# Prompt attention and the sample tokens' cache units as one 16-step software pipeline, with TensorE, VectorE and ScalarE held to the order of the text

## The chip, the cores and the metric

The kernel runs on one core of one Trainium2 chip. The metric is the device time of one execution in microseconds (us). The engines are called PE (TensorE, matrix products and transposes), DVE (VectorE), ACT (ScalarE), POOL (GpSimd, which here issues indirect DMA copies) and SP (SyncE, which issues the other DMA copies). Each engine works through its own queue in order and waits on semaphores that other engines and DMA transfers raise.

## The reference, cut to what matters

One layer of a hybrid decoder: a half-step FFN, a token mixer with 4 GLA heads and 4 MLA heads, an output projection, a second half-step FFN. The change touches the MLA heads only: causal attention of a prompt of 1024 positions, and attention of 8 sample tokens over 4096 cached positions each, which lie in pages.

```python
def mla_prompt_attention(q_nope, q_pe, lat, k_pe, w_uk, w_uv):
    k_nope = jnp.einsum('btc,chd->bthd', lat, w_uk)
    v = jnp.einsum('btc,chd->bthd', lat, w_uv)
    ...
        s = (jnp.einsum('bqhd,bkhd->bhqk', qn, k_nope)
             + jnp.einsum('bqhr,bkr->bhqk', qp, k_pe)).astype(jnp.float32) * MLA_SCALE
        s = jnp.where(kpos[None, :] <= qpos[:, None], s, -jnp.inf)
        p = jax.nn.softmax(s, axis=-1)
        return jnp.einsum('bhqk,bkhd->bqhd', p.astype(v.dtype), v)

def mla_sample_attention(past_lat, past_pe, q_nope, q_pe, lat, k_pe, w_uk, w_uv):
    lat_all = jnp.concatenate([past_lat.astype(lat.dtype), lat], axis=1)
    pe_all = jnp.concatenate([past_pe.astype(k_pe.dtype), k_pe], axis=1)
    q_lat = jnp.einsum('bqhd,chd->bqhc', q_nope, w_uk)
    s = (jnp.einsum('bqhc,bkc->bhqk', q_lat, lat_all)
         + jnp.einsum('bqhr,bkr->bhqk', q_pe, pe_all)).astype(jnp.float32) * MLA_SCALE
    p = jax.nn.softmax(s, axis=-1)
    o_lat = jnp.einsum('bhqk,bkc->bqhc', p.astype(lat_all.dtype), lat_all)
    return jnp.einsum('bqhc,chd->bqhd', o_lat, w_uv).reshape(B, T, MLA_WIDTH)
```

## The kernel before

Every fp32 operand of a prompt product is split into two parts that the PE takes at one pass each: `split` (L90 on ACT for the upper part `_h`, L91 on DVE for the rest `_l`), and `mm3` (L99) adds three products of such parts. The stage concerned begins after the last GLA transpose (L976, `on`) and ends at the first matmul of the output projection (`pr<-ym_h`, L99), which reads the attention's result `ym`.

**Prompt.** The loops run over pairs of heads `t`, heads `hh` and blocks `m` of 256 queries; `scores(m)` projects the queries (`ps<-qn`, then `q_h`, `q_l`), and for each of two row tiles of 128 queries multiplies with keys up to the diagonal in chunks of at most 512 (`sc`, L1381 to L1387: five matmuls and, on the diagonal, a mask), takes the maximum (L1389), the exponential with its sum (L1396), the reciprocal (L1401), and multiplies by it (L1402, DVE). `outputs` of the block before transposes the probabilities (L1417), splits them (`pT_h`, `pT_l`) and multiplies by the values (`po`), and the result is split into `ym`. A pair of heads starts with its rotary queries (`rope`: four ACT copies `sw`, three DVE operations, then `qs`), its values `v` and, for each head, its keys `k`.

**Sample tokens.** 16 units `(g, u)`: four tokens times one eighth of the cache. `prepare` issues eight indirect copies on POOL (L1169: four of `kvt`, four of `pet`) and four DVE transposes in blocks of 32 (`kT` L1171, `peT` L1173). `dec_unit` multiplies (L1198, 48 small matmuls), takes maximum and exponential (L1182, L1183), transposes the probabilities by matmuls with a selector (L1204, 32), copies them on ACT (L1205, `dpT`), multiplies by the cache (L1208, 32) and copies out (L1209, `oc`). `decode(2)` runs two units ahead of the prompt; after that `decode(1)` stands behind each block `m`. `prepare` of the next unit is called behind each unit; tiles `kvt` and `pet` have three buffers, of which a unit takes two.

**Order.** The text gives the dependencies; within them a scheduler decides by its own model in which order the instructions stand in each engine's queue, with `high_priority` on the splits of `pT`. Behind the attention come the GLA results: `yraw` is loaded (its buffer is held by a one-element POOL copy until a block of head 2 is done, L1461), split into `yg`, and then the first tiles of `w_out` are split (`wh`, `wl`). The tiles `raw` (four buffers) are shared by all these loads.

Of the kernel before, what the change touches and what calls it, by code (L numbers as in the profile page):

```python
# [10 lines left out]
F32 = mybir.dt.float32  # L11
# [5 lines left out]
OP = mybir.AluOpType  # L17
# [56 lines left out]
def hybrid_step(ctx: ExitStack, tc: tile.TileContext, I, O, C):  # L74
# [1068 lines left out]
    uv = ep.tile([P, 4, P], F32, name="uv", bufs=1)  # L1143
    ld.dma_start(uv, w_uv)
# [42 lines left out]
    def dec_unit(g, u):  # L1187

        if u == 0:
            grp[g] = (ep.tile([P, 3, NU + 1], F32, name="stat", tag="stat"), ep.tile([P, NU + 1, P], F32, name="oc", tag="oc", bufs=1))  # L1190
        oc = grp[g][1]
        kvs, kts, pts = ready.pop((g, u))
        d = dbank("dsc")
        sc, pTp, po = d[:, :P], d[:, P:384], d[:, 384:]
        steps = [(qbl, kts, cb) for cb in range(4)] + [(qbp, pts, cb) for cb in range(2)]
        for n, (q_, k_, cb) in enumerate(steps):
            for bi in range(4):
                PE.matmul(sc[rows[bi]].rearrange("p (j k) -> p j k", j=J), q_[:, 4 * g + bi, cb], k_[bi][:, :, 32 * cb:32 * cb + 32],  # L1198
                          start=n == 0, stop=n == 5)
        pp = ep.tile([P, P], F32, name="dpp", tag="dpp")  # L1200
        softmax(g, u, sc, P, pp)
# [3 lines left out]
        S.activation(dpT.rearrange("p j t r -> p (j t) r")[:, :, :16], pTp.rearrange("p (x r) -> p x r", r=16), AF.Copy)  # L1205
        for j in range(J):
            for bi in range(4):
                PE.matmul(po[rows[bi]], dpT[:, j, bi], kvs[bi][:, j], start=j == 0, stop=j == J - 1)  # L1208
        S.activation(oc[:, u], po, AF.Copy)  # L1209

    def dec_combine(g):
# [3 lines left out]
        for bi in range(4):  # L1215
            b = 4 * g + bi
            PE.matmul(p[rows[bi], :NS], qlp[:, b], lat_s, start=True, stop=False)
            PE.matmul(p[rows[bi], :NS], qpp[:64, b], kp_s, start=False, stop=True)
        sn = ep.tile([P, NS], F32, name="sn", tag="sn")
        V.tensor_add(sn, p[:, :NS], newmask[:, g * NS:(g + 1) * NS])  # L1220
        pn = ep.tile([P, NS], F32, name="pn", tag="pn")
        softmax(g, NU, sn, NS, pn)
        p = dbank()
        PE.transpose(p[:NS, :P], pn, ident)
        pnT = ep.tile([NS, P], F32, name="pnT", tag="pnT", bufs=1)
        V.tensor_copy(pnT, p[:NS, :P])
        p = dbank()
        PE.matmul(p[:, :P], pnT, latn_s, start=True, stop=True)
        V.tensor_copy(oc[:, NU], p[:, :P])

# [4 lines left out]
        V.transpose(cx[1], cx[0])  # L1235
        V.tensor_reduce(cx[2][:, 16:20], cx[1][:, :16].rearrange("p (a h) -> p h a", h=4), AX.X, OP.min)
        V.tensor_copy(cx[2][:, :16].rearrange("p (a h) -> p a h", h=4),
                      cx[2][:, 16:20].rearrange("p (o h) -> p o h", o=1).to_broadcast([P, 4, 4]))
        V.transpose(cx[3], cx[2])

        S.activation(stat[:, 2, :], stat[:, 0, :], AF.Exp, bias=cx[3][:, 0:1], scale=-1.0)
        V.tensor_mul(stat[:, 1, :], stat[:, 1, :], stat[:, 2, :])
        V.tensor_reduce(cx[2][:, 20:21], stat[:, 1, :], AX.X, OP.add)
# [18 lines left out]
    def decode(n):  # L1262

        for _ in range(min(n, len(units))):
            g, u = units.pop(0)
            dec_unit(g, u)
            if units:
                prepare(*units[0])
# [417 lines left out]
```

## Time and profile before

| what | value |
|---|---|
| median of 3 runs | 2151.42 us (2149.89 to 2153.05) |
| profiled execution | 2162.53 us, span 2160.7 us |
| PE busy | 2013.9 us, 93% |
| DVE busy | 1500.4 us, 69% |
| ACT busy | 818.6 us, 38% |
| POOL busy | 194.2 us, 9% |

The span is the traced part of the profiled execution; busy times are shares of it. Times in the trace count from the span's start. "Idle before" names what a waiting engine waited for; "remote" is a completion of another engine whose instruction had ended earlier than its semaphore came, "issue" a time in which nothing is shown that the engine waited for. PEclk is the clock granted to the PE, as a share of full speed.

### The profile page before, as it was taken

How to read it: one execution, taken by the hardware profiler on the slowest of the kernel's cores; microseconds unless marked ns; L12 is line 12 of the kernel's file. 1: busy time of each engine (PE TensorE's matmuls, PEld its weight loads, DVE VectorE, ACT ScalarE, POOL GpSimd, SP SyncE). 2: the span in 40 equal slices, each digit the busy share in tenths (PEclk: the TensorE clock that was granted, in tenths of full speed). 3: DMA queues.
4: the chain of work that ended last, by engine and by line, in shares of the span. 5: the costliest groups of instructions: out<-in, count | busy, mean ns of one | idle time of the engine just before them, and what ended most of it. 6: DMA issues, size and time to landing. Idle time of an engine off the chain costs nothing. (4 is left out here: it accounts for less than half of the span.)

```text
span 2160.7 us, 41324 instructions
## 1 busy us (share of the span) xinstructions
PE 2013.9 (93%) x16808; PEld 1909.6 (88%) x16808; DVE 1500.4 (69%) x2925; ACT 818.6 (38%) x1555; POOL 194.2 (9%) x225
## 2 busy tenths in 40 slices
PE   7999999999999999897477778899999999999997
PEld 7999999999999988886255657699999999999997
DVE  6877777784968575765455556477777777776776
ACT  6423323244446223456322434344332232333534
POOL 1000000000000012112543341000000000000000
PEclk9999999999999999999688899899999999999999
DMA  6232232377445321022422331643332332475352
GB/s 205 71 121 91 88 123 84 94 228 237 133 130 147 84 73 32 21 88 63 140 83 80 103 104 59 191 147 113 108 90 87 119 94 87 145 259 165 115 154 94
DMA packets 205438, 251.31 MB, mean 116 GB/s; under 512 B 23352, under 2 KB 165984, under 8 KB 205248
## 3 DMA queue, kind: packets, MB, share of 16 engines
q1 hardware_dynamic: 197056, 223.49, 33.6%
q0 software_dynamic: 8192, 25.17, 3.7%
q8 instruction: 132, 2.16, 0.4%
q14 instruction: 58, 0.48, 0.1%
HBM read 189.32 MB, written 59.30 MB: 115 GB/s over the span
## 5 line engine op out<-in xcount | busy, mean ns | idle before, releaser
L99 PE MATMUL pp<-bh,ah 128*128 128x260 f32 (+1 forms) x2432 | 688.0, 283 | 3.8 <-ACT bh L90 3.3
L99 PE MATMUL pp<-bl,ah 128*128 128x260 f32 (+1 forms) x2432 | 688.7, 283 | 1.3 <-DVE bl L91 1.3
L99 PE MATMUL pp<-bh,al 128*128 128x260 f32 (+1 forms) x2432 | 689.6, 284 | 0.2 <-DVE al L91 0.2
L99 PEld LDWEIGHTS pp<-bh,ah 128*128 128x128 f32 x2432 | 460.2, 189 | 4.1 <-ACT bh L90 3.5
L99 PEld LDWEIGHTS pp<-bl,ah 128*128 128x128 f32 x2432 | 459.3, 189 | 1.7 <-DVE bl L91 1.7
L99 PEld LDWEIGHTS pp<-bh,al 128*128 128x128 f32 x2432 | 459.5, 189 | 0.6 <-DVE al L91 0.6
L415 PE MATMUL pp<-tl,dh 128*128 128x256 f32 x1232 | 248.8, 283 | 0.1
L415 PE MATMUL pp<-th,dh 128*128 128x256 f32 (+1 forms) x1232 | 248.7, 283 | 0.0
L415 PE MATMUL pp<-th,dl 128*128 128x256 f32 x1232 | 248.5, 282 | 0.0
L90 ACT ACTIVATE ah<-raw 128x512 fp32r<-128x512 f32 x208 | 129.1, 628 | 258.6 <-PE pp L99 244.2
L415 PEld LDWEIGHTS pp<-tl,dh 128*128 128x128 f32 x1232 | 190.0, 188 | 2.5 <-DVE tl L91 2.4
L415 PEld LDWEIGHTS pp<-th,dh 128*128 128x128 f32 x1232 | 190.7, 189 | 0.1
L415 PEld LDWEIGHTS pp<-th,dl 128*128 128x128 f32 x1232 | 189.7, 188 | 0.2 <-DVE dl L91 0.2
L91 DVE TENSOR_TENSOR al<-raw,ah 128x512 fp32r<-128x512 f32 x208 | 142.4, 688 | 63.7 <-ACT ah L90 63.4
L90 ACT ACTIVATE dh<-a 128x1024 fp32r<-128x1024 f32 (+1 forms) x84 | 83.0, 989 | 249.5 <-PE pp L415 228.0
L91 DVE TENSOR_TENSOR dl<-a,dh 128x1024 fp32r<-128x1024 f32 (+1 forms) x84 | 95.2, 1134 | 113.8 <-ACT dh L90 107.3
L90 ACT ACTIVATE ah<-sl 128x512 fp32r<-128x512 f32 x132 | 83.1, 631 | 214.4 <-PE pp L99 162.2
L99 PE MATMUL pw<-xh,wh 128*128 128x260 f32 (+4 forms) x320 | 100.9, 315 | 0.0
L99 PE MATMUL pw<-xl,wh 128*128 128x260 f32 (+4 forms) x320 | 99.8, 312 | 0.0
L99 PE MATMUL pw<-xh,wl 128*128 128x260 f32 (+4 forms) x320 | 99.5, 311 | 0.0
L91 DVE TENSOR_TENSOR tl<-traw,th 128x1032 fp32r<-128x1032 f32 (+1 forms) x84 | 95.5, 1137 | 3.0 <-ACT th L90 2.7
L91 DVE TENSOR_TENSOR al<-sl,ah 128x512 fp32r<-128x512 f32 x132 | 90.4, 687 | 7.6 <-ACT ah L90 3.8
(433 smaller groups left out, 3642.6 us busy)
## 6 DMA issues: line engine op xcount, KB each, us to landing
traw<-td SPq DMA_DIRECT2D x70, 516.0 KB
raw<-in_ffn_w_gate_dram SPq DMA_DIRECT2D x52, 512.0 KB
raw<-in_ffn_w_up_dram SPq DMA_DIRECT2D x52, 512.0 KB
a<-in_ffn_w_down_dram SPq DMA_DIRECT2D x40, 512.0 KB
td<-q SPq DMA_DIRECT2D x22, 520.0 KB
td<-q SPq DMA_DIRECT2D x22, 512.0 KB
raw<-in_w_out_dram SPq DMA_DIRECT2D x16, 512.0 KB
td<-q SPq DMA_DIRECT2D x22, 260.0 KB
```

The lines of the kernel that those rows point to most:

```text
L90: S.activation(out_h, src, AF.Copy)
L91: eng.tensor_sub(out_l, src, out_h)
L99: PE.matmul(ps, w_, x_, start=i == 0, stop=i == n - 1)
L415: PE.matmul(bank[c][m], w_[:, kk, ms], x_[:, kk, c * N[0]:c * N[0] + N[c]], start=first and j == 0 and (c == 1 or m % 2 == 0), stop=last a ...
```

## The change

`prepare` becomes `fetch` (the eight copies) and `turn` (one DVE transpose); `kvt` gets four buffers, `pet` two. `dec_unit` becomes four parts, and the closing work of a group (`dec_own`, `dec_combine`) generators, which `tick` advances. No unit runs ahead of the prompt: there is one `fetch` there, and 16 steps `(h, m)` follow, each with one unit, the scores of its block and the products of the block before (`old`). A step's text interleaves them. The factor of the softmax is applied by ACT (`scale`) in place of DVE. Probabilities lie in tiles of 512 (six buffers) in place of 1024 (three); the values, keys and rotary queries have one buffer over all heads; values beyond the first two blocks, keys of the second half and the next head's keys are made inside the steps. Tables of the rotary part and `w_uv` come into `raw` tiles. At the end every instruction of PE, ACT and DVE in this part gets a dependency without a semaphore on the one before it in the text, so that the scheduler leaves their order alone. Names of the changed kernel's lines: L1167 `fetch`, L1176 `turn`, L1181 and L1423 maxima, L1425 and L1441 sums of two chunks, L1435 memset, L1443 reciprocal, L1447 `scale`.

```diff
-        W = 512 if tag == "pp" else BL
-        w = pool_.tile([P, 2 * W], F32, name="ropew", tag=tag, bufs=3 if tag == "pp" else 1)
+        W = 512 if tag == "raw" else BL
+        w = rawp.tile([P, 2 * W], F32, name="ropew", tag="raw") if tag == "raw" else pool_.tile([P, 2 * W], F32, name="ropew", tag=tag, bufs=1)
...
-    def prepare(g, u):
-
-        kvs, kts, pts = [], [], []
+    def fetch(g, u):
+
+        got = []
         for b2 in range(2):
-            kvt = ep.tile([P, 2, J, P], F32, name="kvt", tag="kvt", bufs=3)
-            pet = ep.tile([P, 2, J, 64], F32, name="pet", tag="pet", bufs=3)
+            kvt = ep.tile([P, 2, J, P], F32, name="kvt", tag="kvt", bufs=4)
+            pet = ep.tile([P, 2, J, 64], F32, name="pet", tag="pet", bufs=2)
             for bi in range(2):
                 b = 4 * g + 2 * b2 + bi
                 off = bass.IndirectOffsetOnAxis(ap=idx[:, u, b:b + 1], axis=0)
                 for t_, rows in ((kvt[:, bi], kv_rows), (pet[:, bi], pe_rows)):
                     GP.indirect_dma_start(out=t_.rearrange("p j c -> p (j c)"), out_offset=None, in_=rows, in_offset=off)
-            kT = ep.tile([P, 2, J, P], F32, name="kT", tag="kT", bufs=2)
-            V.transpose(kT.rearrange("p b j c -> p (b j c)"), kvt.rearrange("p b j c -> p (b j c)"))
-            peT = ep.tile([P, 2, J, 64], F32, name="peT", tag="peT", bufs=2)
-            V.transpose(peT.rearrange("p b j c -> p (b j c)"), pet.rearrange("p b j c -> p (b j c)"))
-            for bi in range(2):
-                kvs.append(kvt[:, bi])
-                kts.append(kT[:, bi])
-                pts.append(peT[:, bi])
-        ready[g, u] = kvs, kts, pts
+            got.append((kvt, pet))
+        ready[g, u] = got, []
+
+    def turn(g, u, i):
+
+        got, out = ready[g, u]
+        src = got[i // 2][i % 2]
+        t_ = ep.tile(list(src.shape), F32, name=("kT", "peT")[i % 2], tag=("kT", "peT")[i % 2], bufs=2)
+        V.transpose(t_.rearrange("p b j c -> p (b j c)"), src.rearrange("p b j c -> p (b j c)"))
+        out.append(t_)
...
-    prepare(*units[0])
-    decode(2)
+    fetch(*units[0])
...
+    traced = tc.nc.cur_bb.bb.instructions
+    first = len(traced)
...
+    def tick():
+        for _ in range(2):
+            if slack and next(slack[0], slack) is slack:
+                slack.pop(0)
...
-                    V.reciprocal(mx[:, 6:7], tot)
-                    V.tensor_scalar_mul(pp[:, :keys], pp[:, :keys], mx[:, 6:7])
...
-            for m in range(4):
-                prs = scores(m)
-                if pend:
-                    outputs(*pend)
-                pend = (m, prs, h, hh, v_h, v_l)
-                decode(1)
...
+    def scale(pps, mx):
+        for pp, n in pps:
+            S.activation(pp[:, :n], pp[:, :n], AF.Copy, scale=mx[:, 6:7])
...
+    load_uqr(0)
+    rotary(0, 0)
+    load_uk(0)
+    keys(0, 0)
+    load_uv(0)
+    values(0, 0)
+    values(0, 1)
+    rotary(0, 1)
+    load_uq(0)
+    queries(0, 0)
+    for i in range(4):
+        turn(*units[0], i)
+
+    steps = [(h, m) for h in range(4) for m in range(4)]
+    old = None
+    for i, (h, m) in enumerate(steps):
+        g, u = units[i]
+        after = units[i + 1] if i + 1 < len(units) else None
+        new = steps[i + 1] if i + 1 < len(steps) else None
+        if after:
+            fetch(*after)
+        s0 = scores(h, m, 0)
+        dec_scores(g, u)
+        maximum(*s0)
+        if m == 3 and h < 3:
+            load_uk(h + 1)
+            if h == 1:
+                load_uqr(1)
+                load_uv(1)
+            else:
+                load_uq(h + 1)
+        pr0 = exps(*s0, 0)
+        dec_softmax(g, u)
+        tick()
+        if after:
+            turn(*after, 0)
+        s1 = scores(h, m, 1)
+        maximum(*s1)
+        factor(*s0)
+        if old:
+            old.turn(0)
+            old.turn(1)
+            old.part(0)
+            old.part(1)
+        tick()
+        dec_turn(g, u)
+        pr1 = exps(*s1, 1)
+        if after:
+            turn(*after, 1)
+        tick()
+        if m == 3 and h == 1:
+            rotary(1, 0)
+        if old:
+            old.product(0)
+            old.turn(2)
+            old.part(2)
+        scale(pr0, s0[1])
+        factor(*s1)
+        tick()
+        if i and h % 2 == 0:
+            values(h // 2, 2 * m)
+        if after:
+            turn(*after, 2)
+        if old:
+            old.product(1)
+            old.turn(3)
+            old.part(3)
+        if u == 0:
+            while slack:
+                tick()
+        dec_values(g, u)
+        tick()
+        scale(pr1, s1[1])
+        if i and h % 2 == 0:
+            values(h // 2, 2 * m + 1)
+        if m == 1:
+            keys(h, 1)
+        if m == 3 and h < 3:
+            keys(h + 1, 0)
+            if h == 1:
+                rotary(1, 1)
+                load_uq(2)
+        if after:
+            turn(*after, 3)
+        if old:
+            old.product(2)
+        tick()
+        if new:
+            queries(*new)
+        if old:
+            old.product(3)
+            old.out()
+        old = Values(h, m, (pr0, pr1))
+        if u == NU - 4:
+            slack.append(dec_own(g))
+        if u == NU - 1:
+            slack.append(dec_combine(g))
+    old.turn(0)
+    old.turn(1)
+    old.part(0)
+    old.part(1)
+    tick()
+    for j in range(4):
+        old.product(j)
+        old.turn(j + 2)
+        tick()
+        old.part(j + 2)
+        tick()
+    old.out()
+    while slack:
+        tick()
+    uv = rawp.tile([P, 4, P], F32, name="uvr", tag="raw")
+    ld.dma_start(uv, w_uv)
     for h in range(4):
         p = dbank()
         PE.matmul(p[:, :NS], uv[:, h], oT[:, :, h], start=True, stop=True)
         split(ym_h[:, h, SEQ:], ym_l[:, h, SEQ:], p[:, :NS])
+    last = {}
+    for ins in list(traced[first:]):
+        if ins.engine in (mybir.EngineType.PE, mybir.EngineType.Activation, mybir.EngineType.DVE):
+            if ins.engine in last:
+                tc.add_manual_dep(ins, last[ins.engine].name, mybir.DependencyInfo(
+                    mybir.DependencyClass.NoSync, mybir.DependencyReason.DATA), reason="in the order of the text")
+            last[ins.engine] = ins
```

Between the GLA part and the prompt (DVE; a piece of the difference, where `-` is before and `+` the change, a row without a sign stands in both; `lat` and `kp` are the latent and the rotary key, `uql` the rest of the projection's weight):

```order
 L91 TENSOR_TENSOR lat_l<-raw,lat_h 128x1024
-L1171 STREAM_TRANSPOSE kT<-kvt 128x1024
-L1173 STREAM_TRANSPOSE peT<-pet 128x512
 L91 TENSOR_TENSOR kp_l<-raw,kp_h 128x1024
-L1171 STREAM_TRANSPOSE kT<-kvt 128x1024
-L1182 TENSOR_REDUCE stat<-dsc 128x1
-L1173 STREAM_TRANSPOSE peT<-pet 128x512 x2
-L1298 CAST identb<-ident 128x128
-L1299 CAST causalb<-causal 128x128
+L1317 CAST identb<-ident 128x128
+L1318 CAST causalb<-causal 128x128
 L91 TENSOR_TENSOR uql<-uqr,uqh 128x256
```

The transposes and the maximum of the first units no longer stand between the splits of the prompt's inputs.

Inside the stage, DVE, before: from one unit's first `kT` to its `peT`, beside products of the block before:

```order
L1171 STREAM_TRANSPOSE kT<-kvt 128x1024
L91 TENSOR_TENSOR pT_l<-ps,pT_h 128x512 x2
L1404 MEMSET pp 128x128
L1401 RECIPROCAL mx<-mx 128x1
L1402 TENSOR_SCALAR pp<-pp,mx 128x256
L91 TENSOR_TENSOR pT_l<-ps,pT_h 128x512
L1171 STREAM_TRANSPOSE kT<-kvt 128x1024
L1182 TENSOR_REDUCE stat<-dsc 128x1
L91 TENSOR_TENSOR ym_l<-po,ym_h 128x256
L1173 STREAM_TRANSPOSE peT<-pet 128x512 x2
```

And after, in step (1, 2), from the maximum of the first row tile to the second transpose of the next unit's cache:

```order
L1423 TENSOR_REDUCE mx<-sc 128x1 x2
L1425 TENSOR_TENSOR mx<-mx 128x1
L1435 MEMSET pp 128x128
L1181 TENSOR_REDUCE stat<-dsc 128x1
L1176 STREAM_TRANSPOSE kT<-kvt 128x1024
L1423 TENSOR_REDUCE mx<-sc 128x1 x2
L1425 TENSOR_TENSOR mx<-mx 128x1
L1441 TENSOR_TENSOR mx<-mx 128x1
L1443 RECIPROCAL mx<-mx 128x1
L91 TENSOR_TENSOR pT_l<-ps,pT_h 128x512 x2
L1176 STREAM_TRANSPOSE peT<-pet 128x512
```

The multiplications by the factor (L1402) are gone from DVE; `kT` of the next unit stands right behind this unit's maximum, ahead of the second row tile's maximum, and each `peT` several rows behind its `kT`.

POOL, the eight copies of one unit with what they wait for (DMASW: earlier copies; DVE: the transpose that frees a `pet`; PE: the values that free a `kvt`), before:

```order
L1169 DMA pet<-in_cache_pe_dram,idx 128x256 [waits DMASW0_49,DVE_49]
L1169 DMA pet<-in_cache_pe_dram,idx 128x256 [waits DMASW1_49]
L1169 DMA pet<-in_cache_pe_dram,idx 128x256 [waits DMASW2_49,DVE_49]
L1169 DMA pet<-in_cache_pe_dram,idx 128x256 [waits DMASW3_49]
L1169 DMA kvt<-in_cache_kv_dram,idx 128x512 [waits DMASW4_49,PE_49]
L1169 DMA kvt<-in_cache_kv_dram,idx 128x512 [waits DMASW5_49]
L1169 DMA kvt<-in_cache_kv_dram,idx 128x512 [waits DMASW6_49,PE_49]
L1169 DMA kvt<-in_cache_kv_dram,idx 128x512 [waits DMASW7_49]
```

And after:

```order
L1167 DMA pet<-in_cache_pe_dram,idx 128x256 [waits DMASW1_49,DMASW0_49,DVE_49]
L1167 DMA pet<-in_cache_pe_dram,idx 128x256
L1167 DMA kvt<-in_cache_kv_dram,idx 128x512 [waits DMASW2_49,PE_49]
L1167 DMA kvt<-in_cache_kv_dram,idx 128x512 [waits DMASW3_49]
L1167 DMA kvt<-in_cache_kv_dram,idx 128x512 [waits DMASW4_49,PE_49]
L1167 DMA kvt<-in_cache_kv_dram,idx 128x512 [waits DMASW5_49]
L1167 DMA pet<-in_cache_pe_dram,idx 128x256 [waits DMASW7_49,DMASW6_49,DVE_49]
L1167 DMA pet<-in_cache_pe_dram,idx 128x256
```

The two copies of the first `pet` are followed by those of the first `kvt`, and those of the second `pet` come last.

Where the attention ends, ACT, before:

```order
L90 ACTIVATE pT_h<-ps 128x512
L90 ACTIVATE ym_h<-pd 128x8 x2
L90 ACTIVATE yg_h<-yraw 128x1024 x3
L1396 ACTIVATE pp,mx<-sc,mx 128x512 x2
L90 ACTIVATE ym_h<-po 128x256
L90 ACTIVATE yg_h<-yraw 128x1024
L90 ACTIVATE yg_h<-yrs 128x4x8
L90 ACTIVATE pT_h<-ps 128x512 x4
L90 ACTIVATE wh<-raw 128x1024 x2
```

And after:

```order
L1447 ACTIVATE pp<-pp,mx 128x512 x2
L90 ACTIVATE ym_h<-po 128x256
L90 ACTIVATE pT_h<-ps 128x512 x2
L1265 ACTIVATE stat<-stat,cx_15271 128x9
L90 ACTIVATE pT_h<-ps 128x512 x2
L90 ACTIVATE ym_h<-po 128x256
L90 ACTIVATE ym_h<-pd 128x8 x4
L90 ACTIVATE yg_h<-yraw 128x1024 x4
L90 ACTIVATE yg_h<-yrs 128x4x8
L90 ACTIVATE wh<-raw 128x1024 x3
```

All splits of `yg` and the first of `w_out` stand behind the last `ym_h`; before, three `yg_h` stood ahead of the last exponentials and two `wh` ahead of the last `ym_h`.

## Rows read from the trace of the kernel before

**Rows 1.** The page's span in 40 equal slices: busy tenths of the PE and its granted clock.

```profile
PE   7999999999999999897477778899999999999997
PEclk9999999999999999999688899899999999999999
```

**Rows 2.** Busy time of the engines in stretches of the stage. Columns: stretch, its length, busy us of PE, PEld, DVE, ACT and POOL (instructions), granted clock, share of the DMA engines, GB/s.

```profile
1022.00:1088.00 66.00, 31.02 (x329) 20.92 (x330) 30.77 (x55) 24.36 (x63) 32.22 (x33) 0.62 0.40 126
1088.00:1200.00 112.00, 83.16 (x940) 64.29 (x940) 59.90 (x148) 31.97 (x98) 45.80 (x48) 0.86 0.29 88
1200.00:1300.00 100.00, 76.71 (x888) 58.84 (x888) 57.67 (x124) 37.78 (x99) 39.18 (x42) 0.89 0.33 103
1300.00:1340.00 40.00, 34.49 (x450) 27.80 (x450) 26.78 (x74) 15.38 (x45) 7.98 (x10) 0.91 0.25 74
```

**Rows 3.** The waits from 1022 to 1368 us: engine, tile and line that waited, what for; us in all, times, longest.

```profile
POOL pet L1169 <- DVE peT L1173: 88.0, 14, 11.3
ACT dpT L1205 <- remote: 40.1, 11, 6.2
...
DVE kT L1171 <- DMA kvt<-in_cache_kv_dram,idx: 29.6, 15, 3.1
...
PE dsc L1208 <- ACT dpT L1205: 24.5, 9, 4.4
...
PE dsc L1198 <- DVE kT L1171: 13.8, 6, 3.7
```

**Rows 4.** The timeline of the stage's beginning: start, us, engine, line, operation, [idle before <- releaser].

```profile
1021.06 0.86 PE L976 MATMUL ps<-ident,on 128*128 128x128 f32 x2 [0.80 <-ACT on L973]
...
1029.83 1.24 SPq L1307 DMA_DIRECT2D uqr<-in_mla_w_uq_dram  x2
...
1034.48 0.42 ACT L90 ACTIVATE uqh<-uqr 128x256 fp32r<-128x256 f32 x1 [4.59 <-DMA uqr<-in_mla_w_uq_dram]
...
1058.20 0.59 ACT L801 ACTIVATE sw<-ps 32x512 f32<-32x512 f32 x1
...
1087.82 0.39 PE L1381 MATMUL sc<-k_h,q_h 128*128 128x256 f32 x1
```

**Rows 5.** The timeline of the last cache copies of the stage, and the transpose that reads them.

```profile
1322.79 0.98 POOL L1169 DMA_INDIRECT kvt<-in_cache_kv_dram,idx  x1 [3.46 <-DMA yraw<-ygs]
...
1324.07 0.95 POOL L1169 DMA_INDIRECT kvt<-in_cache_kv_dram,idx  x1 [0.31 <-DVE mx L1389]
...
1328.20 1.25 DVE L1171 STREAM_TRANSPOSE kT<-kvt 128x1024 f32<-128x1024 f32 x1 [0.95 <-DMA kvt<-in_cache_kv_dram,idx]
```

**Rows 6.** Groups of instructions from 1088 to 1340 us, shapes apart: busy us, mean ns of one | idle before.

```profile
L1171 DVE STREAM_TRANSPOSE kT<-kvt 128x1024 f32<-128x1024 f32 x25 | 31.1, 1244 | 20.2 <-DMA kvt<-in_cache_kv_dram,idx 14.4 <-PE dsc L1198 5.5
L91 DVE TENSOR_TENSOR pT_l<-ps,pT_h 128x512 fp32r<-128x512 f32 x33 | 21.9, 681 | 15.5 <-ACT pT_h L90 12.2 <-ACT dpT L1205 2.4 <-issue 0.8
L90 ACT ACTIVATE pT_h<-ps 128x512 fp32r<-128x512 f32 x33 | 19.2, 596 | 20.2 <-PE ps L1417 19.3 <-issue 0.4 <-ACT pp L1396 0.3
L1173 DVE STREAM_TRANSPOSE peT<-pet 128x512 f32<-128x512 f32 x25 | 16.4, 686 | 0.0
L1389 DVE TENSOR_REDUCE mx<-sc 128x1 f32<-128x512 f32 x21 | 14.4, 685 | 21.6 <-PE sc L1385 10.0 <-remote 8.5 <-PE sc L1387 3.0
L1401 DVE RECIPROCAL mx<-mx 128x1 f32<-128x1 f32 x29 | 4.5, 154 | 4.5 <-ACT pp L1396 4.2
L1328 DVE TENSOR_TENSOR qs<-qpr,qs 64x512 fp32r<-64x512 f32 x4 | 2.7, 686 | 0.1
```

**Rows 7.** The timeline around the selector's matmuls of two units: one while POOL issues copies, one while it issues none.

```profile
1122.71 0.94 POOL L1169 DMA_INDIRECT pet<-in_cache_pe_dram,idx  x1 [5.05 <-DVE peT L1173]
...
1122.75 0.65 PE L1204 MATMUL dsc<-dsel,dpp 128*32 128x64 f32 x32
...
1126.45 0.94 POOL L1169 DMA_INDIRECT pet<-in_cache_pe_dram,idx  x1 [0.30 <-issue]
...
1127.07 0.38 ACT L1205 ACTIVATE dpT<-dsc 128x256 f32<-128x256 f32 x1 [4.75 <-remote]
...
1320.08 0.66 PE L1204 MATMUL dsc<-dsel,dpp 128*32 128x64 f32 x32
...
1320.80 0.38 ACT L1205 ACTIVATE dpT<-dsc 128x256 f32<-128x256 f32 x1 [0.45 <-PE dsc L1204]
```

**Rows 8.** The timeline of the stage's end.

```profile
1348.46 3.00 ACT L90 ACTIVATE yg_h<-yraw 128x1024 fp32r<-128x1024 f32 x3
...
1352.91 1.23 DVE L91 TENSOR_TENSOR yg_l<-yraw,yg_h 128x1024 fp32r<-128x1024 f32 x1
...
1355.34 1.38 PE L1417 MATMUL ps<-ident,pp 128*128 128x128 f32 x6 [4.05 <-DVE pp L1402]
...
1363.27 0.29 PE L99 MATMUL po<-pT_h,v_l 128*128 128x256 f32 x1
...
1363.59 2.00 ACT L90 ACTIVATE wh<-raw 128x1024 fp32r<-128x1024 f32 x2 [2.38 <-PE po L99]
...
1367.48 0.77 PE L99 MATMUL pr<-ym_h,wh 128*128 128x512 f32 x1 [3.92 <-issue]
...
1368.04 0.63 PE L99 MATMUL pr<-ym_l,wh 128*128 128x512 f32 x1
...
1368.47 0.63 PE L99 MATMUL pr<-ym_h,wl 128*128 128x512 f32 x1
```

More of the change, by code (lines that the diff above doesn't have):

```diff
@@ L1205, in dec_unit, with dec_values @@
         S.activation(dpT.rearrange("p j t r -> p (j t) r")[:, :, :16], pTp.rearrange("p (x r) -> p x r", r=16), AF.Copy)
+    def dec_values(g, u):
+        d, kvs, _ = live.pop((g, u))
+        po = d[:, 384:]
+        if u == 0:
+            grp[g][1] = ep.tile([P, NU + 1, P], F32, name="oc", tag="oc", bufs=1)
         for j in range(J):
@@ L1260, in hybrid_step @@
     units = [(g, u) for g in range(2) for u in range(NU)]
[L1262 to L1267, printed above, removed]
-                prepare(*units[0])
-            if u == NU - 1:
-                dec_combine(g)
-    prepare(*units[0])
-    decode(2)
+    fetch(*units[0])
     close(gw_cm)
@@ new lines, in load_uk, with load_uv @@
+    def load_uk(h):
+        ukr = ap_.tile([P, P], F32, name="ukr", tag="ukr", bufs=1)
+        ld.dma_start(ukr, w_uk[:, h])
+        UK[h] = [ap_.tile([P, P], F32R, name=f"uk_{z}", tag=f"uk_{z}", bufs=1) for z in "hl"]
+        split(*UK[h], ukr)
+    def load_uv(t):
+        uvr = rawp.tile([P, 2, P], F32, name="uvr", tag="raw")
+        ld.dma_start(uvr, w_uv[:, 2 * t:2 * t + 2])
+        UV[t] = [ap_.tile([P, 256], F32R, name=f"uv_{z}", tag=f"uv_{z}", bufs=1) for z in "hl"]
+        split(*UV[t], uvr.rearrange("p h d -> p (h d)"))
@@ new lines, in values, with keys, queries @@
+    def values(t, j):
+        js, (uv_h, uv_l) = slice(j * P, (j + 1) * P), UV[t]
+        p = bank()[:, :256]
+        for i, (l_, r_) in enumerate(((lat_h, uv_h), (lat_l, uv_h), (lat_h, uv_l))):
+            PE.matmul(p, l_[:, js], r_, start=i == 0, stop=i == 2)
+        split(v_h[:, j], v_l[:, j], p)
+    def keys(h, b):
+        s = slice(b * 512, b * 512 + 512)
+        p = bank()
+        mm3(p, [(*UK[h], lat_h[:, s], lat_l[:, s])])
+        split(k_h[:, s], k_l[:, s], p)
+    def queries(h, m):
+        p = bank()[:, :256]
+        wt, s = W[h], QB[m]
+        mm3(p, [(wt[0][:, k], wt[1][:, k], qn_h[:, k, s], qn_l[:, k, s]) for k in range(2)])
+        Qm[h, m] = [ap_.tile([P, 256], F32R, name=f"q_{z}", tag=f"q_{z}") for z in "hl"]
+        split(*Qm[h, m], p)
@@ new lines, in factor, with __init__, turn, part @@
+    def factor(parts, mx):
+        tot = mx[:, 3:4]
+        if len(parts) == 2:
+            V.tensor_add(mx[:, 5:6], mx[:, 3:4], mx[:, 4:5])
+            tot = mx[:, 5:6]
+        V.reciprocal(mx[:, 6:7], tot)
+    def scale(pps, mx):
+        for pp, n in pps:
+            S.activation(pp[:, :n], pp[:, :n], AF.Copy, scale=mx[:, 6:7])
+    class Values:
+        def __init__(self, h, m, prs):
+            self.h, self.m, self.prs, self.n = h, m, prs, m + 1
+            self.ps, self.pts, self.po = {}, {}, None
+        def turn(self, j):
+            if j < self.n:
+                p = self.ps[j] = bank().rearrange("p (j q) -> p j q", j=2)
+                for jj in range(2):
+                    for qi in range(2):
+                        k = (2 * j + jj) * P
+                        PE.transpose(p[:, jj, qi * P:(qi + 1) * P], self.prs[qi][k // 512][0][:, k % 512:k % 512 + P], ident)
+        def part(self, j):
+            if j < self.n:
+                t = self.pts[j] = [ap_.tile([P, 2, 256], F32R, name=f"pT_{z}", tag=f"pT_{z}", bufs=3) for z in "hl"]
+                split(*t, self.ps[j])
+        def product(self, j):
+            if j >= self.n:
+                return
+            if j == 0:
+                self.po = pso.tile([P, 512], F32, name="po", tag="po")[:, :256]
+            vs = slice((self.h % 2) * P, (self.h % 2 + 1) * P)
+            pt_h, pt_l = self.pts[j]
+            for jj in range(2):
+                k = 2 * j + jj
+                for i, (w_, x_) in enumerate(((v_h, pt_h), (v_h, pt_l), (v_l, pt_h))):
+                    PE.matmul(self.po, w_[:, k, vs], x_[:, jj], start=k + i == 0, stop=k == 2 * self.n - 1 and i == 2)
+        def out(self):
+            s = slice(self.m * 256, (self.m + 1) * 256)
+            split(ym_h[:, self.h, s], ym_l[:, self.h, s], self.po)
```

204 lines of the change are left out of this document (85 added, 119 removed).

## The prediction

> **What bounds the kernel now.** I read the page's slices first. The PE is busy nine tenths of nearly every slice; only from slice 18 to 25 does it fall to 4 to 8, and there its granted clock falls to 6 to 9 [rows 1]. That is the stage which the change rewrites: 1021.9, the end of the last GLA transpose, to 1367.5, the first matmul of the output projection [rows 4, 8], 345.6 us. The stretches show two parts. Up to 1088 the PE is busy 31.0 of 66 us at a clock of 0.62; afterwards some 77% at 0.86 to 0.91 [rows 2]. The first prompt scores start only at 1087.8 [rows 4]: until then two sample units and the rotary part run, one behind the other. From there to the last block's transposes at 1355.3 [rows 8] 16 blocks take 267.5 us, 16.7 a block.
>
> Per block, from the sums of the last three stretches (252 us, 15.1 blocks) [rows 2]: PE 194.4/15.1 = 12.9 us busy, DVE 144.4/15.1 = 9.6, ACT 85.1/15.1 = 5.6. No engine fills 16.7. The waits say what does: the unit's chain. POOL waits 88.0 us for `peT`, DVE 29.6 for cache copies, ACT 40.1 at `dpT` for completions, the PE 24.5 for `dpT` and 13.8 for `kT` [rows 3]. Of these the PE's waits cost directly; POOL's make the copies, and so the next unit, late.
>
> **The change, part by part.** No multiplication is removed. What can be won is waiting, so I lay the stage of the changed kernel out anew, by its order and the rows' durations.
>
> *Start.* The units that ran ahead are gone from it, with two thirds of the waits before 1088. What remains is a chain: `uqr` is issued at about 1030 (behind the rotary tables now, which need a `raw` buffer), lands as now 4.6 us later, and is split at 1034.5 [rows 4] to 1035.4. Then six matmuls of 512 columns at the low clock, as the first `pr` rows, 0.43 apart [rows 8], 2.6; four `sw` at 0.59 [rows 4], 2.4; three DVE operations at 0.68, 2.0, and the two `qs` rows with ACT in turn, 2.0 (their price is that of `qs`, 0.686 [rows 6]). That is 9 us for a rotary half. Between the halves keys, `w_uv` and two values pass ACT and DVE, about 4 us, and then the second half without its matmuls, 6.4; the queries' weight, six matmuls and `q` close it, 4. 1035.4 + 9 + 4 + 6.4 + 4 = 1059; I take 1060. That is 28 us earlier than now, but with no unit done, where now two are.
>
> *Step.* The cache loop sets the period. From one unit's first `peT`, which frees the first `pet`, POOL issues two `pet` copies and one `kvt` copy, 3 x 1.28; the second `kvt` copy is readable 4.13 us after its start (1324.07 to 1328.20) [rows 5]. Then DVE in its pinned order: `kT` 1.24, the second row tile's maximum (one or two chunks at up to 0.685, mean 1.0, with the joining operation 1.3), the reciprocal 0.15, none to two `pT_l` at 0.68 (mean 1.2), `peT` 0.69 [rows 6], and about 0.4 for semaphores, estimated. Sum 3.84 + 4.13 + 1.24 + 1.3 + 0.15 + 1.2 + 0.69 + 0.4 = 12.95, say 13.0. PE's 12.9 a block at a clock of 0.88 lies just under it, with DVE (less the multiplications L1402 and more for nothing) and ACT far under. ACT takes the multiplications: at most `pT_h`'s 0.6 [rows 6] for each 512, some 1.5 us a step on an engine with 5.6 of 13; hidden while ACT waits, and worth about as much if `pT` waits for it. I cost it at nothing but in the last block.
>
> 15 loops make 195. The step (1, 3) carries both rotary halves of the second pair of heads; in the middle of the pinned queues, with 8 `sw` (4.7), 6 DVE operations (4.1) and four `qs` pairs, it takes 13 more. After the last loop one and a half steps remain without a fetch, about 15. The last block alone, now 8.2 (1355.34 to 1363.56 [rows 8]), takes 10, with its scaling and three transposes in series. From first scores to last product: 195 + 13 + 15 + 10 = 233.
>
> *Friction.* Two terms the walk leaves out. The PE's share of waits at a granted clock of 0.88: had every matmul been on the path, 12.9 x 16 x 0.12 = 25 us; had none, 0. I take 10, since copies and DVE set most of the loop. And late completions: the selector's 32 matmuls started at 1122.75 and took 0.65, but `dpT` started at 1127.07, while POOL issued four copies; with POOL still, `dpT` followed at 0.72 us after the start [rows 7]. In the changed order POOL's last copies come before the selector's matmuls and the next ones wait for a later `peT`, so mostly POOL should be still. Bounds: 0, and a delay of 3 us in each step, of which a bit over half reaches the next loop, 25 us. I take 8.
>
> *End.* Now `yg` is split in the stalls at 1348 to 1355, and 3.9 us lie between last product and projection [rows 8]. Pinned behind the last `ym_h`, the four `yg_h` at 1.0 and `yg_l` at 1.23 [rows 8] hold the four `raw` buffers: the first goes to `yrs`, the second, free after `ym_h` 0.4, the four small splits 0.6, `yg_h` 1.1 and two `yg_l` 2.5, 4.6 us behind the last product, to `w_out`; landing as in [rows 5] 4.1, `wh` 1.0, hops 0.8: 10.5. The loss is 6.6 us.
>
> *Sum.* 1060 + 233 + 10 + 8 + 10.5 = 1321.5 against 1367.5: 46 us less in a span of 2160.7. The median of the runs is 0.9957 of that span, so 45.8 us less than 2151.4: **2106 us**.
>
> **The rivals.**
>
> *Late completions stay* (20%). If POOL is not still when the selector's matmuls run, `dpT`, and behind it in ACT's queue the exponentials and `pT_h`, come 3 us late in every step. In favour: 11 waits and 40.1 us now [rows 3]. Then 25 stand in place of 8, and the step's DVE rows slip too: 2123 to 2135, say 2128.
>
> *The PE becomes the bound at a lower clock* (10%). The pinned PE queue stops briefly between small groups. If that holds the clock at a mean of 0.75 where it is now 0.88, 12.9 x 0.88/0.75 = 15.1 a step, with a wait 15.7: 1.5 more than 14.2 (13.0 and the 18 of friction over 15 loops) in 16 steps, 24 us: 2130. For it: 0.62 in the sparse first part; against it: 0.86 to 0.91 where the PE was busy three quarters [rows 2], which it would be here too (12.9 of 14.2). The Trainium skill, "TensorE: Matmul & The Clock Gate", in "A second HAM failure mode: psum-queue depth-cycling", says that a PE that idles briefly between groups while it cycles PSUM banks swings between the clock's two levels; the trace's swinging mean of 0.86 to 0.91 agrees with it so far.
>
> *Neither friction* (10%): clock near full, POOL still: 18 less, 2088.
>
> *Slower* (14%): the head of a pinned queue. `kT` now stands ahead of the second maximum, and when its copy is late, DVE holds up maximum, `pT_l` and so ACT and PE, where the scheduler had put work that was ready. Every late microsecond of a copy then costs one in each of 15 steps. The gain is used up when a step takes 46/15 = 3.1 us more than 14.2, that is from 17.3 on, or with a copy readable 7.2 us after its start in place of 4.13. For it: now too DVE waits for copies, up to 3.1 us each [rows 3]; POOL's copies leave in closer succession. Against it: a bound on what the copies move, since the last stretch shows 74 to 103 GB/s [rows 2], below the 126 of the first. A step of 18.5 gives 2106 + 4.3 x 15 = 2170.
>
> *The gains cancel* (6%): the start is won, but the first two units were only moved (28 us against 2 x 14.2), and the steps stay at 16 to 17: 2148 to 2155.
>
> **How the numbers follow.** The forecast as walked has 40% (2095 to 2118 by its start, 1052 to 1070, and a friction of 8 to 28); it is the likeliest. The range from 2088 to 2152 leaves out the slower case and a little below, and holds the rest. Under 0.2% (4.3 us) I count as no change. Faster: 40 + 20 + 10 + 10 = 80%; the same: 6%; slower: 14%.
>
> **What would show it.** First scores near 1060 and no sample unit before them; `kT` to `kT` of successive units near 13 to 14.5 us (16.7 now), 26 in step (1, 3); POOL's `pet` copies released by DVE and its idle time under 5 us a step; `dpT` behind the selector's matmuls by under 1 us where POOL is still; ten us between last `po` and first `pr`. Wrong would be: DVE idle at `kT` for copies by 3 us or more in each step (then the pinned queue is the bound), ACT idle at `dpT` "remote" in most steps (late completions), or a granted clock under 0.8 from the first scores on with the PE over 90% busy.

## The result and the profile after

The changed kernel takes 2173.34 us (median, 2172.94 to 2174.2) beside 2152.24 us for the kernel before: a ratio of 1.010, with a 95% interval of 1.0083 to 1.0118. It is slower by 21 us; the prediction was 46 us faster. The profiled execution of the changed kernel took 2174.2 us with a span of 2172.4. That of before (2162.53) lay 10 us above its median, so the two traces differ by only 11.7 us.

The page's slices of the changed kernel, to be held against [rows 1]:

```profile
PE   8999999999999999897577678799999999999997
PEclk9999999999999999999698798899999999999999
```

The hollow of slices 18 to 25 is still there, not shallower. Its landmarks: the first prompt scores start at 1062.18 (1060 predicted), the last product at 1366.84, the first `pr` at 1378.67 against 1367.48 before [rows 8]. That is 11.2 us later, so all of the difference arises here. Stretches of the stage of the changed kernel, columns as in [rows 2]:

```profile
1022.00:1062.00 40.00, 12.32 (x29) 7.61 (x29) 15.74 (x28) 18.62 (x49) 12.51 (x13) 0.59 0.51 161
1062.00:1160.00 98.00, 76.20 (x877) 58.80 (x877) 51.06 (x106) 35.75 (x100) 41.57 (x44) 0.83 0.29 89
1160.00:1260.00 100.00, 72.65 (x801) 56.76 (x800) 54.91 (x123) 41.40 (x105) 37.29 (x40) 0.83 0.26 80
```

In the two stretches behind the first scores the PE is busy 78% and 73%, at a clock of 0.83: no better than before. The waits from 1022 to 1390 us (us in all, times, longest) say something new:

```profile
POOL pet L1167 <- DVE peT L1176: 105.9, 11, 26.5
ACT dpp L1182 <- DVE stat L1181: 50.3, 14, 5.5
DVE stat L1181 <- PE dsc L1199: 48.8, 14, 5.7
...
PEld dsc L1199 <- issue: 31.8, 40, 1.3
PE dsc L1199 <- issue: 23.7, 35, 1.1
...
PE pd L1280 <- DVE om L1273: 8.2, 2, 4.2
...
ACT dpT L1213 <- PE dsc L1212: 7.2, 4, 2.8
```

The "remote" wait of `dpT` (40.1 us in [rows 3]) is gone, and so is every wait of `kT` for a copy. In their place DVE's unit maximum (`stat`) waits 48.8 us for the 48 score matmuls of the unit, and the PE and its weight loads (PEld) stand still inside them with nothing shown that they wait for ("issue"). One such run in the timeline (start, us, engine, line, operation, [idle before <- releaser]):

```profile
1164.88 0.94 POOL L1167 DMA_INDIRECT kvt<-in_cache_kv_dram,idx  x1 [1.08 <-PE dsc L1222]
...
1169.88 0.95 POOL L1167 DMA_INDIRECT pet<-in_cache_pe_dram,idx  x1 [0.30 <-issue]
1170.02 1.08 PE L1199 MATMUL dsc<-kT,qbl 128*32 128x128 f32 x32
1170.91 0.55 PE L1199 MATMUL dsc<-peT,qbp 128*32 128x128 f32 x4
1171.13 0.95 POOL L1167 DMA_INDIRECT pet<-in_cache_pe_dram,idx  x1 [0.30 <-issue]
1171.92 0.28 PE L1199 MATMUL dsc<-peT,qbp 128*32 128x128 f32 x1 [0.46 <-issue]
1172.62 0.27 PE L1199 MATMUL dsc<-peT,qbp 128*32 128x128 f32 x1 [0.42 <-issue]
1173.34 0.61 PE L1199 MATMUL dsc<-peT,qbp 128*32 128x128 f32 x10 [0.45 <-issue]
1173.98 0.29 DVE L1181 TENSOR_REDUCE stat<-dsc 128x1 f32<-128x128 f32 x1 [3.23 <-PE dsc L1199]
```

36 matmuls start within 1.2 us. Then single ones follow at a distance of about 0.70 us, and the last ten run freely from some 1.2 us after the end of POOL's last copy of a burst of six (copies in close succession, 1164.88 to 1172.08). Such a stop is called a hole here. Holes stand in nearly every step with a fetch: of the loads and matmuls of the score runs, 45 start more than 0.3 us after the one before, 33.9 us in all. (One of the 45, 1.4 us in the first unit, stands in all the pinned kernels below, also in those without POOL's copies.) The mean of 13 steps, without the rotary step (1, 3) and the one behind it, is 17.2 us (14.2 predicted).

### The profile page after: what moved, and what is told of

It is laid out like the page before. It is cut to its first block, busy times and chain, and to the rows that moved or that the text cites. A ratio compares the mean times of both kernels' runs of the same rounds, so it can differ in the third digit from the quotient of the medians.

```text
span 2172.4 us, 41324 instructions
## 1 busy us (share of the span) xinstructions
PE 2018.0 (93%) x16808; PEld 1915.0 (88%) x16808; DVE 1495.8 (69%) x2893; ACT 841.4 (39%) x1603; POOL 190.4 (9%) x225
## 3 DMA queue, kind: packets, MB, share of 16 engines
q8 instruction: 132, 2.16, 0.4%
## 4 chain that ended last, share of the span: by engine, by line
PE 85%; DVE 6%; ACT 4%; issue 3%; DMA 1%; POOL 1%; SPq 0%; POOLq 0%; ACTq 0%; DVEq 0%
PE pp L99 41%; PE pp L415 19%; PE pw L99 6%; PE pr L99 4%; PE dsc L1199 2%; PE pw L1043 1%; PE po L1479 1%; PE ps L99 1%; PE dsc L1222 1%; PE pg L941 1%; DVE qt L937 1%; PE sc L1411 1%; DVE pT_l L91 1%; PE sc L1413 1%; PE ps L1462 0%
```

## The experiments

Three questions: do POOL's copies cause the holes, by what of them, and what does the pinned order cost by itself? Times are medians; ratios, with their 95% intervals, are to the kernel before beside the same runs. The kernels with fixed rows or with unit 0's tiles leave out the look-up of the pages, and so compute something else.

**Take the copies away, or give them to SyncE.** The first kernel lets units 1 to 15 read unit 0's tiles; the second copies fixed rows of the same size by plain copies on SP.

```diff
-                for t_, rows in ((kvt[:, bi], kv_rows), (pet[:, bi], pe_rows)):
-                    GP.indirect_dma_start(out=..., out_offset=None, in_=rows, in_offset=off)
+                for t_, rows in ((kvt[:, bi], kv_rows), (pet[:, bi], pe_rows)):
+                    ld.dma_start(t_.rearrange("p j c -> p (j c)"), rows[P * b:P * b + P])
```

> Left out: the cache copies of units 1 to 15; every unit works on the tiles of unit 0. The trace of the changed kernel shows the 48 score matmuls of a unit (L1199) spread over 3.7 to 5.0 us in most steps, with holes of 0.6 to 1.4 us in their second half, where the two units without POOL copies beside them take 1.2 and 2.4 us. Theory A (PE gets small matmuls slowly while POOL issues indirect copies) and theory B (reading peT is slowed by what the copies write to memory) both expect the holes gone, L1199 at 1.2 to 2 us in every step, the steps shorter by 2.5 us or more, the time near 2125 to 2135 (2173 less 14 x 2.6 and what hangs behind). Theory C (the pinned order itself is a chain too long, whatever the PE does) expects the holes to matter little: 2160 or more.

> Changed: the copies are of the same size and go to the same tiles, but come from SP as plain copies of fixed cache rows, not of the rows that the page table names; POOL issues nothing in the steps. Theory A expects the holes in L1199 gone, since POOL is still: as without copies, 2125 to 2140. Theory B expects the holes to stay, since as many bytes land in the same places: 2165 to 2175. If SP's eight issues a step (0.35 us each) delay other loads, a few us on top in either.

Measured: 2106.25 us without copies (0.9768, 0.9752 to 0.9784) and 2101.96 with SP's (0.9748, 0.9732 to 0.9764). But for the one of 1.4 us, the holes are gone in both. The stretch that follows the first scores, first with SP's copies, then without any:

```profile
1062.00:1160.00 98.00, 88.64 (x1272) 71.74 (x1270) 69.64 (x149) 52.47 (x147) 0.00 (x0) 0.97 0.41 126
```

```profile
1062.00:1160.00 98.00, 88.29 (x1270) 71.55 (x1270) 69.86 (x150) 52.51 (x147) 0.00 (x0) 0.97 0.02 6
```

126 GB/s or 6 make no difference, so it is not the bytes. The same 98 us hold 1272 matmuls in place of 877, and the clock is 0.97 in place of 0.83 in the same pinned order. It gained more than I had expected (2125 to 2135): 71 us by the medians, 3.5% by the ratios.

**Copies without indices, by POOL.** As above, with `GP.dma_start` in place of `ld.dma_start`.

> The changed kernel, pinned, with the cache copies as plain copies of fixed rows, but issued by POOL (the output is then not the reference's). Same bytes, same queue of an engine, no indices. Theory I (the toll belongs to copies through indices): 2095 to 2110, no holes of 0.70 us in the run of 48 score matmuls, as with SyncE's plain copies (2102). Theory Q (it belongs to whatever POOL issues in bursts): 2150 to 2175, holes as in the changed kernel (2173).

Measured: 2108.53 us (0.9764, 0.9744 to 0.9785), no holes but the one of 1.4 us. Rows of the two pages, first of the changed kernel, then of this one, and one of this one's timeline:

```profile
q0 software_dynamic: 8192, 25.17, 3.6%
```

```profile
q0 software_dynamic: 8192, 25.17, 3.8%
...
kvt<-in_cache_kv_dram POOLq DMA_DIRECT2D x64, 256.0 KB, 4.0
...
1087.46 2.16 POOL L1166 DMA_DIRECT2D kvt<-in_cache_kv_dram  x4 [0.57 <-PE dsc L1221]
```

Same queue, packets and bytes, without the toll (what the copies cost the kernel). So it is not what every copy from POOL costs. What makes the difference is open, because more than the index changes: four plain copies pass POOL in 2.16 us, 0.54 each, where indirect ones follow at 1.25, so the bursts are shorter in time, and only one of them, of seven copies, covers more than 97 loads and matmuls (129, without a hole). The rows also lie in one piece and not in pages. The Trainium skill, "DMA: Bandwidth & Descriptors" (section "SWDGE vs HWDGE vs iDMA"), says that direct and indirect copies from GpSimd alike have their descriptors made in software and kept in rings in SBUF. If that making of descriptors as such disturbed the PE, plain copies would do it too; here they do not, at their shorter time on POOL.

**Which matmuls are hit.** The six column blocks of a unit's scores in another order:

```diff
-        steps = [(qbl, 0, cb) for cb in range(4)] + [(qbp, 1, cb) for cb in range(2)]
+        steps = [(qbp, 1, cb) for cb in range(2)] + [(qbl, 0, cb) for cb in range(4)]
```

> Changed: in a unit's scores the 16 matmuls with peT come before the 32 with kT (same sum). Theory A expects the holes to stand at the same count as before, from about the 36th matmul of the 48 on, now in the kT part, and the time unchanged within 4 us (2173). Theory B expects them in the first 16, with peT, and none in the kT part; the time about the same or a little better.

Measured: 2177.21 us (1.0092, 1.0075 to 1.0109). Now the `kT` products stall and `peT` runs through:

```profile
1146.71 0.64 PE L1199 MATMUL dsc<-peT,qbp 128*32 128x128 f32 x16
...
1147.17 0.83 PE L1199 MATMUL dsc<-kT,qbl 128*32 128x128 f32 x21
...
1148.84 0.42 PE L1199 MATMUL dsc<-kT,qbl 128*32 128x128 f32 x3 [0.84 <-issue]
```

Place decides, not the operand. Counted in the trace of the changed kernel, the first hole at the score run opens 95 to 131 loads and matmuls after the start of POOL's burst of six. Where a burst covers few and large matmuls, none opens: the burst of four at 1203.08 covers 10 loads and matmuls. Late packets of instructions do not explain most holes: the packets of the page's queue q8 (kind `instruction`, 16 KB, one for about 256 loads and matmuls) take 0.9 to 1.5 us here as with SP's copies, and only 7 of the 45 holes have one under way.

**The pinning alone, and before without the toll.** Leave out the loop that adds the dependencies; in the kernel before, give the copies to SP; then both.

```diff
-    last = {}
-    for ins in list(traced[first:]):
...
-            last[ins.engine] = ins
```

> Undone: the dependencies that pin PE, ACT and DVE to the order of the text; the scheduler orders the same instructions by its own model. Theory C expects a gain of 20 us or more (2150 or less), since ready work can be put ahead of waits. Theory A expects the small matmuls to be cut into shorter runs with prompt matmuls between them, so part of the holes go: 2150 to 2165. If the pinning is what keeps the steps short, the time rises above 2180.

> The kernel before with the same replacement as in the second run: cache copies of the same size as plain copies of fixed rows from SP, POOL issues none. If the toll that POOL's issuing takes of the PE is the same thing that shows in the kernel before as late completions at dpT (40.1 us, 11 waits 'remote'), those waits go and the time falls by 25 to 50 us, to 2105 to 2130, so that the change against it is worth little or nothing. If the late completions of before have another cause, they stay, and only waits for copies can go: 2140 to 2155.

> The changed kernel without the pinning of the three engines, and with the cache copies as plain copies of fixed rows issued by SyncE, so that POOL issues none (the output is then not the reference's). Without POOL's issuing the kernel before took 2073 us and the changed one, pinned, 2102. Theory P (the 29 us are the price of holding the engines to the order of the text): 2070 to 2082. Theory T (they come from the text itself: no unit ahead of the prompt, a closing part behind the last product, single buffers for keys and values): 2093 to 2105, no better than pinned. Each theory expects no holes in the run of score matmuls.

Measured: 2135.2 us unpinned (0.9902, 0.9886 to 0.9919), below the 2150 to 2165 that the holes alone were to give, as theory C had it; 2073.07 for before with SP's copies (0.9613, 0.9596 to 0.963), and 2060.53 for unpinned with SP's (0.9542, 0.9523 to 0.9562). The last two lie 32 and 10 us below the expected ranges. Before with SP's copies, the first two stretches of [rows 2], and its wait at `dpT`:

```profile
1022.00:1088.00 66.00, 43.17 (x586) 32.10 (x587) 44.54 (x87) 31.96 (x87) 0.00 (x0) 0.83 0.57 173
1088.00:1200.00 112.00, 100.53 (x1258) 77.29 (x1260) 84.62 (x198) 51.80 (x140) 0.00 (x0) 0.95 0.37 115
```

```profile
ACT dpT L1204 <- PE dsc L1203: 8.4, 10, 1.6
```

The kernel before pays the toll too, 3.9%; there part of it shows as `dpT` "remote" (40.1 us), which is gone here. So the four corners are, with POOL's indirect copies and with SP's plain ones:

| order | POOL, indices | SP, fixed rows |
|---|---|---|
| before | 2152 | 2073 |
| changed, pinned | 2173 | 2102 |
| changed, unpinned | 2135 | 2061 |

Pinning costs 38 and 41 us, with the toll or without. The text by itself, unpinned, is 0.7 to 1% better than before by the ratios.

**The closing part.** Pinning ended with the sixteenth step, beside SP's copies:

> The changed kernel with SyncE's plain copies of fixed rows (2102; the output is then not the reference's), and the pinning ended with the sixteenth step, so that what closes the attention is left to the scheduler. If the pinned closing costs what it cost beside gated copies, 7 to 9 us, the time is 2093 to 2095; if the other engines were the limit there, 2100 to 2104.

Measured: 2094.81 us (0.9704, 0.9685 to 0.9722), 7 less than 2102. From the first scores of the last block to the last product it now takes 19.1 us, not 24.3.

**Move the copies.** The second half's four copies held behind the unit's maximum and sum, by two-element POOL copies into the tiles; then with the closing part free; then unpinned:

```diff
+            if after is not None:
+                GP.tensor_copy(kvt[:1, :, 0, 0], after)
+                GP.tensor_copy(pet[:1, :, 0, 0], after)
...
         dec_softmax(g, u)
+        if after:
+            fetch(*after, (1,), grp[g][0][:1, 0:2, u])
```

> The changed kernel with the copies of a unit's second half (4 of 8) held back until the unit before has its maximum and sums (a two-element POOL copy from them into each tile), so that beside the 48 score matmuls POOL issues two copies and not six in a row. Theory A in the form that the toll begins only after about 100 PE instructions within one run of POOL copies expects the holes in L1199 mostly gone and the steps at 12 to 15 us: 2120 to 2140. If every copy takes its toll wherever it is issued, the holes move to the selector's or the value matmuls and to their completions: 2160 to 2180.

> As the run before, and the pinning ends with the 16 steps: the last block and the closing of the second group of units are left to the scheduler, so that the splits of yg can stand in their stalls again. Now 24 us lie between the last step's first scores and the last product and 11.8 us between it and the projection. Expected 5 to 10 us less than the run before from the end alone; none if the end is bound by its own chain.

> The unpinned kernel (2135.2 us) with the same hold on the second half's copies. If bursts of copies still cost it (its holes sum to 19 us), it comes to 2115 to 2130. If its scheduler's order has already put other work beside the copies, the hold only makes copies late: 2135 to 2150.

Measured: 2201.88 us (1.0212, 1.0194 to 1.023), 2193.27 (1.017, 1.0152 to 1.0188) and 2147.48 (0.9956, 0.9939 to 0.9973): all slower than without the gate (2173 pinned, 2135 unpinned), and the first above both of its expected ranges. The waits of the first:

```profile
ACT dpT L1217 <- remote: 70.7, 12, 6.8
...
PE dsc L1226 <- ACT dpT L1217: 43.4, 14, 5.3
```

The bursts are still of six, since the next `pet` pair had come free and followed the gated four. They now stand over the selector's matmuls and the values, and the toll moved there: in the score runs only the hole of 1.4 us is left.

**Half the copies.** Only `kvt` by indirect copies; `pet` stays unit 0's.

> The changed kernel, pinned, with POOL's indirect copies, but only those of kvt: units 1 to 15 take the pet tiles of unit 0 (the output is then not the reference's). 64 + 4 indirect copies in place of 128, in bursts of at most four in place of six, two thirds of the bytes. POOL's copies cost the changed kernel 67 to 71 us in all (2173 against 2102 and 2106). Theory L (a price for each copy): about half stays, 2134 to 2142. Theory R (only the part of a burst beyond some three or four copies costs, since the holes open late in a burst): 2105 to 2120, few holes. A price by bytes would leave two thirds: 2148 to 2153.

Measured: 2118.82 us (0.9814, 0.9793 to 0.9836). 17 us above 2102: of the toll a quarter is left, not half. A burst of four, and what it leaves of the score run:

```profile
1127.40 0.95 POOL L1170 DMA_INDIRECT kvt<-in_cache_kv_dram,idx  x1 [0.30 <-issue]
1127.62 0.69 PE L1202 MATMUL dsc<-peT,qbp 128*32 128x128 f32 x7
1129.41 0.49 PE L1202 MATMUL dsc<-peT,qbp 128*32 128x128 f32 x9 [1.10 <-issue]
```

The burst (1123.65 to 1128.35) ends as the holes begin. Counted as above, 9 holes with 6.8 us are left in place of 45 with 33.9. In the five bursts with holes the first opens 109 to 125 loads and matmuls after the burst's start; the bursts without holes cover at most 55.

**All copies, in other bursts.** POOL's queue held to the order of the text as well: in each half `kvt`, `pet`, `kvt`, `pet`. With gate and free closing that makes bursts of four and four; the same with PE, DVE and ACT unpinned; and without gate, pinned, one burst of up to eight.

```diff
-        if ins.engine in (mybir.EngineType.PE, mybir.EngineType.Activation, mybir.EngineType.DVE):
+        if ins.engine in (mybir.EngineType.PE, mybir.EngineType.Activation, mybir.EngineType.DVE, mybir.EngineType.Pool):
```

> Complete computation, three engines pinned for the sixteen steps and free for the closing part, the second half's copies behind the unit's maximum and sum as in the earlier gated kernel (2193 us), but POOL's queue now held to the order of the text too: in each half kvt, pet, kvt, pet. The next unit's first pet pair then no longer joins the gated four; bursts are four and four in place of six and two. Theory S (the toll comes from the part of a burst beyond some four copies): 2095 us without any toll, plus once or twice the 17 us that bursts of four kvt copies cost, 2110 to 2130. Theory N (the number of copies in a step makes the toll, wherever they stand): 2180 to 2200, as the gated kernel.

> The same POOL order and gate, PE, DVE and ACT left to the scheduler, complete computation. Unpinned kernels so far: 2060 us with SyncE's plain copies, 2135 as changed, 2147 with the gate and bursts of six. Theory S: 2060 plus 17 to 40, so 2077 to 2105. Theory N: 2135 to 2150.

> The changed kernel with POOL's queue, too, held to the order of the text (kvt, pet, kvt, pet for each half) and no gate, complete computation: the first pet pair no longer goes ahead by itself, so that most of a unit's copies leave in one burst of six to eight that starts when the values free a kvt buffer. Theory S: a longer burst, more holes, 2175 to 2200. Theory N: the same number of copies in a step, 2165 to 2178, as the changed kernel (2173).

Measured: 2154.24 us (1.000, 0.999 to 1.0011), 2125.89 (0.9858, 0.9837 to 0.9879) and 2209.63 (1.0261, 1.0241 to 1.028). Eight in a burst cost 36 us more than six and two, with 63 holes of 46.8 us in all, and no engine but POOL (0.3 us) waits for a cache copy. Four and four cost 39 less than the gated six (2193): over scores and values together 8 holes of 5.9 us are left of 18 of 12.7, and the late completions at `dpT` halve (first the gated six, then four and four):

```profile
ACT dpT L1217 <- remote: 62.5, 10, 6.8
```

```profile
ACT dpT L1217 <- remote: 31.8, 8, 5.3
```

So for the same number of copies the burst's length counts, and theory N falls. But theory S had 2110 to 2130, 2077 to 2105 and 2175 to 2200, and all three came out above, by 24, 21 and 10 us: a burst of four is not nearly free wherever it stands. The kernel before shows it too: most of its bursts are of four, some only 1.2 to 1.6 us apart, and it loses 79 us. The gated four of the first kernel lie over the selector's matmuls:

```profile
1167.28 0.65 PE L1216 MATMUL dsc<-dsel,dpp 128*32 128x64 f32 x32
...
1169.96 0.95 POOL L1173 DMA_INDIRECT pet<-in_cache_pe_dram,idx  x1 [0.30 <-issue]
1171.95 0.38 ACT L1217 ACTIVATE dpT<-dsc 128x256 f32<-128x256 f32 x1 [3.92 <-remote]
1172.39 0.91 PEld L1226 LDWEIGHTS dsc<-kvt,dpT 128*32 128x32 f32 x32 [2.71 <-ACT dpT L1217]
```

`dpT` comes 4.7 us after the start of matmuls that the trace shows as 0.65 us long, and 1 us after POOL's last copy: the late completion of [rows 7], in the changed kernel. The unpinned version of this, 2125.89 us with all of the computation, is the best found: 1.4% under before.

## Why the prediction was wrong

- **Start: right.** 1062.2 for 1060.
- **Step and walk: the size right without the toll, the reason not.** From the first scores to the last product I had 233 us; with SP's copies it is 237.8, ordinary steps 12.5 us on average for 13.0. But I had the step set by the loop through the copies, 8 of whose 13 us are copies; without any copy the same steps take 12.6 us on average, so that loop does not set them, and that 13.0 came out was luck. Nearest to a bound is the PE, busy 88 of 98 us there, which the prediction had just under the loop (12.9); that it sets the step was not tested. The rotary step takes 29.1 there for 26, and the one behind it 21.5, which I had not priced.
- **Friction: the step that failed.** I had 18 us for clock and late completions, bounds 0 to 50 together. Measured from first scores to last product is 304.7 us, 66.9 more than with SP's copies. That is 49 of the 57 us by which the first `pr` missed its forecast; 4.8 are the walk's, 2.2 the start's, 1.3 the end's. The pair of [rows 7] showed the effect, `dpT` 4.3 us behind its matmuls with POOL issuing and 0.72 with POOL still, and I read it as a price of that tile alone, which the new order would avoid. A wait that [rows 3] leaves out had the same sign (`PE dsc L1208 <- issue: 10.1, 4, 3.7`): all four stand beside a burst of POOL, and with SP's copies none is left. The new order did avoid the late `dpT`: `dpT` has no "remote" wait left. The copies then lay over the next run of small matmuls. The clock's part of the term follows the holes in part: from 1062 to 1160 us it is 0.97 without copies or with SP's, 0.92 with POOL's plain ones and 0.83 with the toll, from 1160 to 1260 us 0.88 to 0.90 without and 0.83 with it. How the 67 us divide into holes (33.9 directly), what waits for them and the lower clock is not separated. By the medians the forecast missed by 67 us (2173 for 2106), 10 more than in the traces: the sum started from a profiled execution 10 us above its median.
- **End: right.** 11.8 us for 10.5; another 5 lie in the pinned closing part ahead of the last product, where `om` (3.06 us) holds up PE's order.
- **The sum's other side.** I took the waits of [rows 3] for waits of the unit's chain, which another order would remove. Without the toll the kernel before is at 2073, faster than the pinned order at 2102: much of what I meant to win by order was the toll, and the pinning gave away 41 us, for which the sum had no term.
- **The rivals.** "Late completions stay" named the right resource, with a price of 25 us at most and in the wrong place. "Slower" had the right sign and a wrong mechanism: no `kT` waited for a copy. (The 74 to 103 GB/s given there for "the last stretch" are the last two of [rows 2].) "PE bound at a lower clock" needed the PE over 90% busy; it was 73 to 78%. On this the Trainium skill, "TensorE: Matmul & The Clock Gate", in "A second HAM failure mode: psum-queue depth-cycling", puts the swings of the clock in one kernel down to a PE that idles briefly between groups while it cycles through PSUM banks. The same pinned order with the same bank use was granted 0.97 from 1062 to 1160 us once POOL issued no copies, so most of the loss of clock in that stretch came with the holes. In the next stretch 0.88 to 0.90 is all that comes back, and the cause of the rest is open.

## What to carry to other kernels

Where an engine waits for "remote" or "issue" in runs of small matmuls, look at what POOL does at that time before reordering anything; a kernel with the indirect copies replaced by plain ones of the same size prices the interference in one run. If they must be indirect, let the bursts lie over few, large matmuls and keep them short; shorter bursts gained here, but they are not free, as the kernel before shows. Write a pipeline's text, but test the pinning by itself: here the text won about 1% and the pinning lost 2%.

## What the runs showed of the hardware

POOL's indirect copies (1.25 us apart) slow the PE's small matmuls, also those that do not read what the copies write: starts 0.70 us apart in place of about 0.03, from some 95 to 131 loads and matmuls after the start of a burst of six until 1.2 to 1.3 us after it ends, where the run of matmuls lasts so long. It looks as if the PE drew on a stock that is not refilled meanwhile; what the stock is was not shown, and that it is the instruction packets is unlikely (7 of 45 holes). Plain copies from POOL through the same queue, 0.54 us apart (2108 us), and 126 GB/s of SP's copies (2102 us) do not do it. Over the stage of 16 units, 128 such copies cost 3.5 to 3.9% of the kernel; the holes that are seen stand late in each burst.
